# A decoder trunk on one core: at the phase changes of the mix stage, the second tile's opening weights are split right behind the first tile's first product, and the norm's two vectors are loaded in the last phase

## The chip, the cores and the metric

The kernel runs on one core of one Trainium2 chip. The metric is the device time of one execution in microseconds (us). A core has a matrix engine (PE, with its weight loads shown apart as PEld), three other compute engines that work beside it (DVE, ACT, POOL), and queues that start memory transfers; nearly all transfers of this kernel are started by the queue of SP. Each engine takes its instructions in the order in which the built program holds them, and an instruction that waits holds up everything behind it on its engine.

## The reference

One decoder layer on 2048 rows of 1024 float32 values:

```python
u = x * (1.0 + scale) + shift                      # scale, shift, gate from SiLU(c) @ w_ada + b_ada
q, k, v, a_gate, p_in, p_gate, m_a, m_p = split(u @ w_in)
a = (sliding_window_sink_attention(q, k, v) * silu(a_gate)) @ w_attn_proj
p = ((multiscale_causal_pool(p_in) @ w_pool_mix * pool_scale) * silu(p_gate)) @ w_pool_proj
y = (sigmoid(m_a) * a + sigmoid(m_p) * p) @ w_out * (1.0 + gate)
x = layer_norm(alpha * x + y, ln_gain, ln_bias)
```

The last three lines are the kernel's mix stage. `ln_gain` and `ln_bias` are the two vectors of the norm.

## The kernel before

**Products.** A float32 operand is held as two float32r parts: hi, a rounded copy that ACT makes (`CAST`), and lo, the rest, which DVE makes by subtraction (`low`, line 132). A product is hi x hi, hi x lo and lo x hi over four blocks: 12 matmuls of 128x512, the lo part of the weights in the last four. Two by two blocks are multiplied with seven products in place of eight, by sums and differences of blocks: on the activations' side there are seven sets, `B11 T1 T2 B21 T3 B22 T4`, on the weights' side a `Quad`.

**Tiles.** One `Quad` is what the change calls a tile. Its raw weights lie in `W` (four blocks) and `A22`. POOL makes the sums and differences of the blocks in place: `sum1` (line 266) before the first use, `mid` (lines 270 and 271) and `late` (line 275). `pair_split` splits two blocks at once into two buffers `w_set` (cast on line 303, subtraction on line 132). A tile has an opening pair (for the products with `B11` and `T1`), a second pair (for `T2` and `B21`) and a third (for `T3` and `B22`); `half_split` (line 310) does the single block for `T4`. There are four `w_set` buffers, so a pair can be split only when a pair split earlier has been used up by PE.

**Order of the products.** A group is two tiles. `back` does the later products of a group: T2, B21 of tile 1, T2, B21 of tile 2, then T3 and B22 of each, at last T4 of tile 1 and T4 of tile 2. `front` does the opening ones of the next group: B11, T1 of tile 1, B11, T1 of tile 2. Results are drained by DVE a product or two later (`two_behind`).

**Phases.** The mix stage has six: the end of the second half's gates, attention projection and pool projection for the first half of the rows, the same two for the second half, and the output projection with the norm. At each of the five phase changes (called seams 1 to 5 below) the seven sets change as well. `set_steps` loads a set by SP into the lo half of its place, ACT casts it, DVE subtracts (in the profile `set_B<-set_B`, `set_T<-set_T`, 128x1024); `set_steps` gives each step a place in a list counted in products, `hooks` runs it there. So at a seam DVE has three kinds of work: splitting weights, splitting sets, and draining results (`g<-mm,g`, `g<-lg,g`, `wide<-g,wide`, 128x512).

**Who sets the order.** `ring` runs the groups of a phase and calls `after`, which at a seam is the list of two `front` calls that the change replaces; inside a phase the next group's fronts are called in `ring` itself. `tick` runs the hooks and what `defer` put off. Instructions called through `act`, `dve`, `pool`, `sp` and `pe` (the class `Ordered`, line 57 in the profile) keep their written order; those called as `nc.scalar`, `nc.vector`, `nc.gpsimd`, `nc.sync` may be shifted among them by the framework's scheduler, so that one moved call can change more than its own place.

**The norm's vectors.** `vectors` loads gain and bias (512 KB each, spread over 128 partitions) into `wide0` and `wide1`; `hooks` puts it in the last group of phase 4 (the pool projection of the second half). They are first read in `norm_row`'s `power` and `scale`. `load_z` loads rows of x (`in_xr`) to `wide2` to `wide7`.

## Time and profile before

| what | us |
|---|---|
| median of three runs | 1679.81 |
| lowest and highest of them | 1678.58, 1680.28 |
| the profiled execution, its own time | 1682.07 |
| its span, first to last instruction | 1680.3 |
| busy in the span: PE | 1643.7 |
| busy: DVE, ACT, POOL | 1205.1, 1025.5, 957.7 |
| mean granted PE clock (1 is full) | 0.996 |

The mix stage runs from about 1150 us to the end. A row of the timeline gives start, duration, engine, line, operation, written tile and read tiles, shape, count, and in brackets the time that the engine sat idle before it and what ended that. Rows that follow each other are merged where their shapes agree, so one row can stand for several instructions. A duration includes what an instruction lost to others while it ran; the step from one start to the next on a busy engine is what it really took from that engine. A row of the windows view gives for one stretch the time that an engine was busy and how many instructions it began (in brackets), the granted PE clock, the share of time that the 16 transfer engines were busy, and GB/s.

### The profile page before, as it was taken

The page shows a single profiled execution, that of the slowest core. Times are in us where ns is not written, and L with a number is a line of the kernel's source. Part 1 is how long each engine was busy: PE and PEld are TensorE (multiplying, and loading weights), DVE is VectorE, ACT ScalarE, POOL GpSimd, SP SyncE. Part 2 cuts the span into 40 slices and gives each one's busy share as a digit, 9 for nine tenths or more (in the row PEclk, how much of TensorE's full clock was granted, in tenths as well). Part 3 has the DMA queues.
Part 4 walks back from the last instruction along what each step waited for, and adds up shares of the span by engine and source line. Part 5 has one row for each costly group of instructions (what it writes and reads, how often), then busy time and mean ns, then how long its engine had stood idle before and what let it go on. Part 6 is the DMA issues. An engine that isn't in the chain of part 4 may idle for free.

```text
span 1680.3 us, 24675 instructions
## 1 busy us (share of the span) xinstructions
PE 1643.7 (98%) x8058; PEld 1384.1 (82%) x8058; DVE 1205.1 (72%) x2156; ACT 1025.5 (61%) x2146; POOL 957.7 (57%) x710
## 2 busy tenths in 40 slices
PE   7999999999999999999999999999999999999997
PEld 6788888888888788888888888888888878887886
DVE  6944646676867866566567677777769896978777
ACT  4754547778778755334577777776647455544452
POOL 3343437585867838773376858597355563324442
PEclk9999999999999999999999999999999999999999
DMA  9588743243543588872432345335968886677443
GB/s 362 210 295 288 206 156 126 99 127 107 173 137 113 189 269 302 318 270 98 153 128 88 126 131 169 120 126 188 328 229 303 288 310 215 218 261 252 153 148 113
DMA packets 185970, 331.56 MB, mean 197 GB/s; under 512 B 18016, under 2 KB 43760, under 8 KB 185840
## 3 DMA queue, kind: packets, MB, share of 16 engines
q1 hardware_dynamic: 182720, 325.72, 57.0%
q10 hardware_dynamic: 3088, 4.23, 1.1%
q8 instruction: 64, 1.05, 0.3%
q14 instruction: 66, 0.54, 0.1%
q0 software_dynamic: 32, 0.02, 0.0%
HBM read 223.77 MB, written 109.28 MB: 198 GB/s over the span
## 4 chain that ended last, share of the span: by engine, by line
PE 84%; DVE 7%; DMA 4%; issue 2%; ACT 2%; POOL 2%; SPq 0%; POOLq 0%; DVEq 0%; ACTq 0%
PE mm L57 53%; PE lg L57 24%; PE pv L57 4%; PE pt L57 4%; DMA head_T<-in_wada_dram 1%; DVE L L57 1%; DVE w_set L132 1%; DVE set_T L57 1%; DMA head_B<-in_wada_dram 1%; DVE room L57 1%; DMA g<-mp_d 0%; DVE w_set L57 0%; DVE wide L57 0%; ACT L L57 0%; ACT w_set L57 0%
## 5 line engine op out<-in xcount | busy, mean ns | idle before, releaser
L57 PE MATMUL mm<-set_B,w_set 128*128 128x512 f32 x2664 | 654.6, 393 | 5.7 <-DVE w_set L132 5.4
L57 PEld LDWEIGHTS mm<-set_B,w_set 128*128 128x128 f32 x2664 | 496.6, 188 | 108.7 <-DVE w_set L132 6.3
L57 PE MATMUL mm<-set_T,w_set 128*128 128x512 f32 x1824 | 454.9, 396 | 2.1 <-DVE mm L57 1.2
L57 PE MATMUL lg<-set_T,w_set 128*128 128x512 f32 x1704 | 408.6, 390 | 2.1 <-DVE w_set L132 0.6
L57 PEld LDWEIGHTS mm<-set_T,w_set 128*128 128x128 f32 x1824 | 337.6, 189 | 71.5 <-DVE mm L57 4.2
L57 PEld LDWEIGHTS lg<-set_T,w_set 128*128 128x128 f32 x1704 | 318.8, 188 | 70.4 <-DVE w_set L132 1.1
L132 DVE TENSOR_TENSOR w_set<-W,w_set 128x1024 fp32r<-128x1024 f32 x137 | 194.7, 1421 | 145.7 <-ACT w_set L303 136.8
L303 ACT CAST w_set<-W 128x1024 fp32r<-128x1024 f32 x137 | 143.8, 1050 | 194.2 <-PE mm L57 134.2
L57 POOL TENSOR_TENSOR w_set<-W,w_set 128x512 fp32r<-128x512 f32 x120 | 158.9, 1332 | 109.6 <-ACT w_set L57 107.8
L266 POOL TENSOR_TENSOR W<-W,A 128x512 f32<-128x512 f32 x46 | 71.5, 1555 | 261.7 <-DMA A<-in_win_dram 42.8
L57 POOL TENSOR_TENSOR W<-W 128x512 f32<-128x512 f32 x82 | 111.0, 1368 | 52.8 <-DVE sm L57 25.8
L57 DVE TENSOR_TENSOR o<-pv,o 64x128 f32<-64x128 f32 x256 | 71.9, 281 | 96.6 <-ACT o L57 93.2
L270 POOL TENSOR_TENSOR W<-W 128x512 f32<-128x512 f32 x44 | 85.3, 1941 | 96.6 <-DVE w_set L132 75.6
L57 ACT ACTIVATE L<-L,nm 128x257 f32<-128x257 f32 (+1 forms) x256 | 127.2, 498 | 17.8 <-DVE nm L57 8.5
L275 POOL TENSOR_TENSOR W<-W 128x512 f32<-128x512 f32 x46 | 73.1, 1589 | 94.2 <-DVE w_set L132 84.3
L57 DVE CUSTOM_DVE_ANT_0 L<-lg,bt,nsink 128x256 f32<-128x256 f32 (+1 forms) x256 | 111.7, 474 | 15.0 <-DMA pg<-pg_d 10.2
L57 ACT CAST w_set<-W 128x512 fp32r<-128x512 f32 (+1 forms) x165 | 101.5, 629 | 24.5 <-POOL W L57 14.5
L57 ACT COPY o<-pv 64x256 f32<-64x256 f32 x128 | 47.4, 370 | 70.0 <-PE pv L57 68.7
L57 POOL TENSOR_TENSOR spare<-spare 128x512 f32<-128x512 f32 x48 | 84.1, 1760 | 9.4 <-ACT spare L57 7.1
L57 ACT ACTIVATE L<-L,sm 128x256 f32<-128x256 f32 (+1 forms) x128 | 64.3, 502 | 36.9 <-DVE sm L57 36.5
L57 DVE TENSOR_TENSOR ptl<-pt,pth 128x512 fp32r<-128x512 f32 (+1 forms) x128 | 85.7, 669 | 1.0 <-ACT pth L57 0.9
L271 POOL TENSOR_TENSOR W<-W 128x512 f32<-128x512 f32 x44 | 66.8, 1519 | 28.0 <-DMA W<-in_win_dram 20.8
(234 smaller groups left out, 2409.8 us busy)
## 6 DMA issues: line engine op xcount, KB each, us to landing
W<-in_win_dram SPq DMA_DIRECT2D x42, 512.0 KB, 5.9
W<-in_win_dram SPq DMA_DIRECT2D x42, 256.0 KB, 4.1
A<-in_win_dram SPq DMA_DIRECT2D x42, 256.0 KB, 5.0
ag_d<-sig SPq DMA_DIRECT2D x32, 256.0 KB, 5.7
pg_d<-sig SPq DMA_DIRECT2D x32, 256.0 KB, 4.4
pg<-pg_d SPq DMA_DIRECT2D x32, 256.0 KB, 3.4
pin_B<-fin SPq DMA_DIRECT2D x32, 256.0 KB, 2.0
ag<-ag_d SPq DMA_DIRECT2D x32, 256.0 KB, 3.1
```

The lines of the kernel that those rows point to most:

```text
L57: return lambda *args, **kw: self.tc.keep_in_program_order(op(*args, **kw))
L132: engine.tensor_tensor(dst, src, as32(hi), ALU.subtract)
L266: e.tensor_tensor(self.w[:, 1, :], self.w[:, 2, :], self.a22, ALU.add)
L270: e.tensor_tensor(x[:, 1, :], x[:, 1, :], x[:, 0, :], ALU.subtract)
L271: e.tensor_tensor(x[:, 2, :], x[:, 0, :], x[:, 2, :], ALU.subtract)
L275: e.tensor_tensor(x[:, 3, :], x[:, 3, :], x[:, 1, :], ALU.subtract)
L303: a.copy(by_two(hi), raw)
```

## The change

A new function `fronts` takes the place of the two `front` calls at a seam. It hands `front` of tile 1 a function that splits tile 2's opening pair; `front` calls it behind the product with `B11` and ahead of the `tick` that runs that product's hooks. Before, tile 2's pair was split only after both products of tile 1 with both their ticks. The front of tile 2 then takes that pair and makes only its `mid` sums. Fronts inside a phase are as they were.

`vectors` moves from the last group of phase 4 to the output phase, position 3 of its first group, counted in products.

```diff
--- before.py
+++ after.py
@@ -325,11 +325,13 @@
                     skip_group_check=True,
                 )
 
-    def front(ph, q, tick):
-        w = pair_split(ph, q.first())
+    def front(ph, q, tick, w=None, then=None):
+        w = w or pair_split(ph, q.first())
         q.mid()
         a, b = bank(), bank()
         product(a, w[0], "B11", True)
+        if then:
+            then()
         tick()
         product(b, w[1], "T1", True)
         tick()
@@ -412,6 +414,11 @@
             q.consume(ph, 1, 0, c)
         defer(1, lambda: use_up(1))
         defer(2, use_up)
+
+    def fronts(ph, grp, tick):
+        early = []
+        first = front(ph, grp[0], tick, None, lambda: early.append(pair_split(ph, grp[1].first())))
+        return [first, front(ph, grp[1], tick, early[0])]
 
     def finish_pairs(ph, grp, opened, tick):
 
@@ -1621,20 +1628,19 @@
             if i + 1 < len(phases):
                 planned(hooks, ph, phases[i + 1][1], True, groups=groups)
                 nxt = phases[i + 1][0][0]
-                after = lambda tick, nxt=nxt: [front(ph, q, tick) for q in nxt]
+                after = lambda tick, nxt=nxt: fronts(ph, nxt, tick)
             else:
+                def vectors():
+                    for name, src in (("gain", gain), ("lnb", lnb)):
+                        vec[name] = wide(ph, len(vec))
+                        sp.dma_start(vec[name], src.partition_broadcast(P))
+
+                hooks.setdefault((0, 3), []).append(vectors)
                 for at, row in ((1, 2), (1, 3), (5, 4), (5, 5)):
                     hooks.setdefault((0, at), []).append(lambda row=row: load_z(ph, row))
             if i in (3, 5):
                 ta.clear()
             if i == 4:
-
-                def vectors():
-                    for name, src in (("gain", gain), ("lnb", lnb)):
-                        vec[name] = wide(ph, len(vec))
-                        sp.dma_start(vec[name], src.partition_broadcast(P))
-
-                hooks.setdefault((-1, 5), []).append(vectors)
                 hooks.setdefault((-1, 7), []).append(lambda: [load_z(ph, row) for row in range(2)])
             opened = ring(ph, groups, opened, hooks, nxt, after, i == 5)
 
```

What the built program makes of it is shown at three places. The first is DVE at seam 3 (first half's pool projection to second half's attention projection), from the split of the second half of the set T2 on. `w_set` rows are weights: numbers 14055 before and 14027 now are the opening pair of tile 2, 14108 is the second pair of tile 1; `g` and `wide` rows drain results. Before:

```order
L57 TENSOR_TENSOR set_T2_234<-set_T2_234 128x2x512
L57 TENSOR_TENSOR g_13822<-mm_13743,g_13822 128x512
L57 TENSOR_TENSOR wide5_12572<-g_13819,wide5_12572 128x512
L57 TENSOR_TENSOR wide6_12573<-g_13822,wide6_12573 128x512
L57 TENSOR_TENSOR set_B21_68<-set_B21_68 128x2x512
L57 TENSOR_TENSOR g_13824<-lg_13827,g_13824 128x512
L132 TENSOR_TENSOR w_set_14055<-W_13926,w_set_14054 128x1024
L57 TENSOR_TENSOR wide7_12574<-g_13824,wide7_12574 128x512
L57 TENSOR_TENSOR set_B21_68<-set_B21_68 128x2x512
L57 TENSOR_TENSOR set_T3_568<-set_T3_568 128x2x512
L132 TENSOR_TENSOR w_set_14108<-W_13891,w_set_14107 128x1024
```

DVE at the same place now:

```order
L57 TENSOR_TENSOR set_T2_234<-set_T2_234 128x2x512
L57 TENSOR_TENSOR g_13822<-mm_13743,g_13822 128x512
L132 TENSOR_TENSOR w_set_14027<-W_13926,w_set_14026 128x1024
L57 TENSOR_TENSOR wide6_12573<-g_13822,wide6_12573 128x512
L57 TENSOR_TENSOR g_13819<-lg_13782,g_13819 128x512
L57 TENSOR_TENSOR wide5_12572<-g_13819,wide5_12572 128x512
L57 TENSOR_TENSOR set_B21_68<-set_B21_68 128x2x512
L57 TENSOR_TENSOR g_13824<-lg_13827,g_13824 128x512
L132 TENSOR_TENSOR w_set_14108<-W_13891,w_set_14107 128x1024
L57 TENSOR_TENSOR wide7_12574<-g_13824,wide7_12574 128x512
L57 TENSOR_TENSOR set_B21_68<-set_B21_68 128x2x512
```

Tile 2's opening pair now stands ahead of the split of B21's first half, tile 1's second pair ahead of the split of B21's second half and of T3, and the drain of `lg_13782` (before: ahead of this piece) behind the opening pair.

The second place is ACT at the same seam, from the cast of tile 1's opening pair on. Before:

```order
L303 CAST w_set_14006<-W_13891 128x1024
L303 CAST w_set_14054<-W_13926 128x1024
L57 CAST set_B21_68<-set_B21_68 128x2x512
L348 COPY lg_14104<-mm_14012 128x512
L57 CAST set_B21_68<-set_B21_68 128x2x512
L349 COPY p5_14103<-mm_14013 128x512
L303 CAST w_set_14107<-W_13891 128x1024
```

ACT there now:

```order
L303 CAST w_set_14006<-W_13891 128x1024
L303 CAST w_set_14026<-W_13926 128x1024
L57 CAST set_B21_68<-set_B21_68 128x2x512 x2
L303 CAST w_set_14107<-W_13891 128x1024
L350 COPY lg_14104<-mm_14012 128x512
L351 COPY p5_14103<-mm_14013 128x512
```

The cast of tile 1's second pair moved ahead of the two copies; that of tile 2's opening pair already stood ahead of B21. On DVE the rows of seam 5 (pool projection to output projection) read as those of seam 3 do, with `w_set_15253` before and `w_set_15227` now for tile 2's opening pair; on ACT at seam 5 the copy to `lg` stays ahead of the cast of tile 1's second pair, and both now stand behind the two casts of B21.

The third place is SP at seam 5, where `W_15089` and `W_15127` (now `W_15123`) are the output projection's first two tiles, `y_d` the mixed rows in memory, and `A22_15394`, `A22_15441` blocks of the two tiles of its second group. Before:

```order
L255 DMA W_15089<-y_d_137 128x4x128 x3
L57 DMA wide0_15122<-in_gain_dram 128x1024
L57 DMA wide1_15124<-in_lnb_dram 128x1024
L57 DMA y_d_137<-wide4_14505 128x512
L255 DMA W_15127<-y_d_137 128x4x128 x3
L57 DMA y_d_137<-wide6_14538 128x512
L57 DMA wide2_15166<-in_xr_dram 128x1024
L57 DMA wide3_15168<-in_xr_dram 128x1024
```

SP there now:

```order
L255 DMA W_15089<-y_d_137 128x4x128 x3
L255 DMA W_15123<-y_d_137 128x4x128
L57 DMA y_d_137<-wide4_14505 128x512
L255 DMA W_15123<-y_d_137 128x4x128 x2
L255 DMA A22_15394<-y_d_137 128x4x128
L255 DMA A22_15441<-y_d_137 128x4x128
L57 DMA y_d_137<-wide6_14538 128x512
L57 DMA wide2_15162<-in_xr_dram 128x1024
```

Gain and bias left this place, and two loads of the second group's blocks came in. The two vectors now stand behind two loads of rows of x and ahead of the loads of the second group's first tile:

```order
L57 DMA wide4_15327<-in_xr_dram 128x1024
L57 DMA wide5_15329<-in_xr_dram 128x1024
L57 DMA wide0_15370<-in_gain_dram 128x1024
L57 DMA wide1_15372<-in_lnb_dram 128x1024
L255 DMA W_15393<-y_d_137 128x4x128 x3
```

On PE and POOL the order of the instructions is the same before and now.

## The prediction

> **What bounds the kernel now.** I read the page's head first, then the chain of waits, the waits of PE, the windows around each wait, and the timeline of the seams.

> ```profile
> span 1680.3 us, 24675 instructions
> PE 1643.7 (98%) x8058; PEld 1384.1 (82%) x8058; DVE 1205.1 (72%) x2156; ACT 1025.5 (61%) x2146; POOL 957.7 (57%) x710
> ```

> PE is busy 98% of the span, so this change can pay only where PE waits in the mix stage or runs slowly. PE's timeline shows three waits at the stretches that the change touches:

> ```profile
> 1227.55 1.21 PE L57 MATMUL lg<-set_T,w_set 128*128 128x512 f32 x4 [0.64 <-DVE w_set L132]
> 1366.21 1.98 PE L57 MATMUL mm<-set_B,w_set 128*128 128x512 f32 x4 [2.33 <-DVE w_set L132]
> 1523.51 2.07 PE L57 MATMUL mm<-set_B,w_set 128*128 128x512 f32 x4 [3.08 <-DVE w_set L132]
> ```

> The second is seam 3, the third seam 5. Both times PE has done eight matmuls of tile 2's first product and waits for the lo part of that tile's opening pair. Seams 1, 2 and 4 show no wait there; the 0.64 comes later in seam 1's group. The windows of PE say what a wait leaves behind (after the count comes the granted clock, then the transfer share):

> ```profile
> 1226.00:1227.50 1.50, 0.90 (x4) 1.00 0.00 0
> 1366.20:1368.00 1.80, 1.79 (x5) 0.54 1.03 381
> 1369.00:1370.00 1.00, 1.00 (x5) 0.63 1.01 342
> 1370.00:1371.00 1.00, 1.00 (x6) 1.00 1.06 408
> 1523.50:1525.00 1.50, 1.50 (x4) 0.50 1.02 325
> 1525.00:1527.00 2.00, 2.00 (x7) 0.56 0.87 259
> ```

> After each long wait PE runs at half clock for some 3 us; the wait of 0.64 leaves the clock at 1.00 in its window. The chain has the price:

> ```profile
> 1366.21 5.52 PE mm L57 x16
> 1371.73 2.72 PE lg L57 x12
> 1523.51 5.45 PE mm L57 x16
> ```

> Twelve matmuls take 2.72 at full clock, or 0.227 each, so sixteen take 3.63, and the two stretches lost 1.89 and 1.82 more.

> **Part 1: tile 2's opening pair, split earlier.** Seam 3 before, on DVE, ACT, PE and POOL:

> ```profile
> 1353.88 1.21 DVE L132 TENSOR_TENSOR w_set<-W,w_set 128x1024 fp32r<-128x1024 f32 x1
> 1353.99 1.05 ACT L303 CAST w_set<-W 128x1024 fp32r<-128x1024 f32 x1 [2.57 <-DVE g L57]
> 1355.18 1.68 POOL L270 TENSOR_TENSOR W<-W 128x512 f32<-128x512 f32 x1 [1.77 <-DVE w_set L132]
> 1355.62 0.68 DVE L57 TENSOR_TENSOR g<-mm,g 128x512 f32<-128x512 f32 x1
> 1361.33 1.06 ACT L57 CAST set_B<-set_B 128x1024 fp32r<-128x1024 f32 x1 [6.28 <-DMA set_B<-ain_B]
> 1361.40 0.68 DVE L57 TENSOR_TENSOR g<-mm,g 128x512 f32<-128x512 f32 x1
> 1361.91 1.98 PE L57 MATMUL mm<-set_B,w_set 128*128 128x512 f32 x8
> 1363.20 1.22 DVE L57 TENSOR_TENSOR set_B<-set_B 128x1024 fp32r<-128x1024 f32 x1
> 1364.94 1.21 DVE L132 TENSOR_TENSOR w_set<-W,w_set 128x1024 fp32r<-128x1024 f32 x1
> 1366.30 6.15 POOL L270 TENSOR_TENSOR W<-W 128x512 f32<-128x512 f32 x1 [9.44 <-DVE w_set L132]
> 1368.95 1.22 DVE L132 TENSOR_TENSOR w_set<-W,w_set 128x1024 fp32r<-128x1024 f32 x1
> ```

> The cast of the pair is done by 1355 (second row); only its subtraction, at 1364.94, is late: it stands behind six drains and the split of B21, whose cast waited for a transfer until 1361.33. In the new order it follows the drain that was at 1361.40. Rows of 128x1024 step by 1.14, rows of 128x512 by 0.60. Two drains that stood ahead of that one now stand behind it or one place on, so I put it 0.6 earlier, at 1360.8, or at worst where it was. The subtraction then ends at 1362.0 to 1362.6. PE wants it at 1361.91 + 8 x 0.227 = 1363.7. The wait of 2.33 goes, and the half clock behind it.

> Can what follows keep up with a PE that is 4.2 us earlier? T2 of tile 1 would start at 1361.91 + 24 x 0.227 = 1367.35 and want the lo part of its pair at 1369.2. DVE in the new order, from 1362.6: two drains and `lg` to 1364.4, half of B21 and a drain to 1366.1, that pair to 1367.3. The margin is 1.9. Then a drain, half of B21 to 1369.0 (wanted about 1371), both halves of T3 to 1371.3, tile 2's second pair to 1372.5, wanted at 1372.8 + 1.8 = 1374.6. That pair also needs POOL's `mid`, which took 6.15 at 1366.30 since DVE ran four rows of two on-chip operands without a gap; at 1355.18, with a drain from the accumulators (`g<-mm`) behind, it took 1.68. In the new order it starts at 1362.6 with the drain of `lg` next, so I take 1.7; even 6.15 would end at 1368.8, before DVE asks. POOL's sum puts about 1.2 on DVE each time that it gets in between. Two such sums leave margins near zero, so I deduct 0.5.

> Seam 5 has the same picture:

> ```profile
> 1511.80 1.21 DVE L132 TENSOR_TENSOR w_set<-W,w_set 128x1024 fp32r<-128x1024 f32 x1
> 1518.07 0.58 ACT L348 COPY lg<-mm 128x512 f32<-128x512 f32 x1
> 1518.45 1.97 PE L57 MATMUL mm<-set_B,w_set 128*128 128x512 f32 x8
> 1518.70 0.68 DVE L57 TENSOR_TENSOR g<-mm,g 128x512 f32<-128x512 f32 x1
> 1522.24 1.21 DVE L132 TENSOR_TENSOR w_set<-W,w_set 128x1024 fp32r<-128x1024 f32 x1
> ```

> The subtraction moves from 1522.24 to behind the drain of 1518.70, which itself comes 0.6 earlier: it ends by 1519.9, and PE wants it at 1518.45 + 1.8 = 1520.3. Here the drain of `lg` moves behind it, to about 1520.4, and ACT's copy to `lg` (1518.07 before) must wait for that drain, until 1521.1 or, with a POOL sum between, 1521.7; behind it on ACT stands the cast of tile 1's second pair, done by 1522.7. T2 would start at 1518.45 + 5.45 = 1523.9, its lo part be wanted at 1525.7 and be done at 1524.5 to 1525.2. Tile 2's second pair is done at 1529.7 to 1531.5 and wanted at 1531.1. Again 0.5 is deducted.

> Seams 1, 2 and 4 have no wait to lose. At seam 1 the pair's cast depends on POOL:

> ```profile
> 1203.63 2.31 DVE L57 TENSOR_TENSOR set_B<-set_B 128x1024 fp32r<-128x1024 f32 x1
> 1204.88 1.05 ACT L303 CAST w_set<-W 128x1024 fp32r<-128x1024 f32 x1 [1.12 <-POOL W L266]
> 1205.97 2.21 DVE L132 TENSOR_TENSOR w_set<-W,w_set 128x1024 fp32r<-128x1024 f32 x1
> ```

> In the new order the split of B21 (first row) stands behind the third row, so DVE idles from 1203.63 to 1205.97, 2.34 us. POOL then works unhindered: both rows last twice their 1.2, so about two POOL sums fall out of DVE's way, 2.3 in return. I take 0, between a gain of the 0.64 and a loss of 2.34. Seams 2 and 4 swap a split and a drain of 0.6 to 1.1, hidden by the fact that PE has no wait there; 0, within 0.6 either way.

> **Part 2: the vectors.** Removed from seam 5 are two issues on SP and their two transfers. The first row is of the chain, the others of the timeline:

> ```profile
> 1497.18 6.32 DMA wide<-in_gain_dram
> ...
> 1497.18 1.31 SPq L57 DMA_DIRECT2D wide<-in_gain_dram  x1
> 1498.54 0.45 SPq L57 DMA_DIRECT2D wide<-in_lnb_dram  x1
> 1502.56 2.73 DVE L132 TENSOR_TENSOR w_set<-A,w_set 128x512 fp32r<-128x512 f32 x2 [0.83 <-ACT w_set L310]
> 1525.96 1.93 SPq L57 DMA_DIRECT2D wide<-in_xr_dram  x2
> 1537.44 0.38 SPq L255 DMA_DIRECT2D W<-y_d  x1
> 1551.43 1.64 DVE L57 SCALAR_TENSOR_TENSOR wide<-wide,mean,wide 128x1024 f32<-128x1024 f32 x1
> ```

> Tile 2's raw weights land earlier, but DVE's row at 1522.24 shows its split late by DVE's own queue and not for want of them: 0. The two block loads that come into this place wait for buffers that DVE frees by 1502.56 + 2.73 = 1505.3, before the store queued next is due: 0. The vectors are issued behind the rows of x, near 1528, and land by 1541 if each takes the 6.3 that the chain gave gain; their first reader comes at 1551.43 - 4.9 = 1546.5. The second group's weights behind them (1537.44) wait for a buffer, not for SP. 0, at worst 1.31 + 0.45 = 1.8.

> **Sum.** 2.33 + 1.89 + 3.08 + 1.82 = 9.1, less 1.0 deducted: 8.1 off. The profiled execution took 1682.07 for a span of 1680.3; it would take 1674.0. The median of the runs shown, 1679.81, lies 2.26 below it, and becomes 1671.7.

> [...] The rows above show the clock halved after waits of 2.33 and 3.08. [...]

> **Rivals.**

> *The waits turn into short ones.* DVE's amount of work is unchanged. If its rows finish no earlier than before, tile 1's second pair is done at 1370.2 and 1527.4, against 1369.2 and 1525.7 wanted: waits of 1.0 and 1.7, short of 2.33. Gain 9.1 - 2.7 = 6.4, or 4.6 if the 1.7 costs clock: 1673.4 to 1675.2. Against it: that pair now stands two or three rows earlier.

> *Nothing to measure.* The transfers, not DVE, set the pace: their share is 1.0 from 1366 on, and a PE that is earlier meets sets that are not. The pull is given back before the seam's group ends: within 3.4 of 1679.81, 1676.4 or more. Against it: with the share at 1.0 PE has no wait between seam 3 and seam 5 in the rows above, and B21's cast ran at 1361.33, nine us ahead of its product.

> *The half clock is not due to the wait.* If the saturated transfers caused it, only 5.4 - 1.0 = 4.4 would go: 1675.4. Against it: at 1370 the share is 1.06 and the clock 1.00.

> [...]

> *Slower.* ACT and DVE take instructions in order, and the early split now heads both queues; where tile 2's sums are late, as at seam 1, everything behind it waits. Price per seam: the idle 2.34 passed on to PE, and 1.9 of clock, 4.2. At seams 1, 2 and 4 together 12.6, less 9.1: 3.5 slower, 1683.3. It decides when all three bite. Only seam 1 shows a late sum.

> **Chances.** A difference under 0.2% (3.4 us) can hardly be told from none. Both waits gone: 0.56, the forecast 1671.7. Short waits: 0.20. Clock unchanged: 0.03. Nothing to measure: 0.12. Slower: 0.09. So faster 0.79, same 0.12, slower 0.09. The range reaches from 1669.3 (all 9.1, and the 0.64, and some scatter) to 1677.0, which takes in the short waits and the edge of no change.

> **What would show it.** Right: PE's waits of 2.33 and 3.08 absent, granted clock 1.00 at both seams, the subtraction of tile 2's opening pair ahead of that of B21, POOL's `mid` near 1.7. Wrong: a new wait of 2 us or more of PE for the second pair or for B21 in the same groups; at seam 1 the 0.64 grown; norm rows waiting for gain.

## The result

| | median, us | lowest and highest | ratio to the kernel before, with its 95% interval |
|---|---|---|---|
| changed kernel, six runs | 1673.78 | 1672.59, 1676.22 | 0.9965 (0.9952 to 0.9977) |
| the same again, five runs | 1675.20 | 1673.98, 1675.91 | 0.9967 (0.9955 to 0.9980) |
| the same once more, six runs | 1674.84 | 1673.96, 1676.78 | 0.9967 (0.9954 to 0.9979) |

Each row was taken beside runs of the kernel before on the same chip, with medians of 1680.12, 1680.26 and 1681.03. So the change makes the kernel faster by 5.1 to 6.3 us, 0.33 to 0.35%. The forecast was 1671.7 with a range of 1669.3 to 1677.0. The profiled execution of the changed kernel took 1675.67 for a span of 1673.9 us.

The profile after: the timeline of seam 3, on DVE, PE, POOL and the weight loads.

```profile
1361.87 1.22 DVE L132 TENSOR_TENSOR w_set<-W,w_set 128x1024 fp32r<-128x1024 f32 x1
1362.70 2.88 PE L57 MATMUL mm<-set_B,w_set 128*128 128x512 f32 x12
1363.17 1.70 POOL L270 TENSOR_TENSOR W<-W 128x512 f32<-128x512 f32 x1 [5.96 <-DVE w_set L132]
...
1367.07 1.21 DVE L132 TENSOR_TENSOR w_set<-W,w_set 128x1024 fp32r<-128x1024 f32 x1
...
1373.32 2.30 DVE L132 TENSOR_TENSOR w_set<-W,w_set 128x1024 fp32r<-128x1024 f32 x1
...
1375.67 0.77 PEld L57 LDWEIGHTS lg<-set_T,w_set 128*128 128x128 f32 x4 [0.54 <-DVE w_set L132]
```

The subtraction of tile 2's opening pair starts at 1361.87 (1364.94 before), and PE runs tile 2's first product as one row of twelve: the wait of 2.33 is gone. POOL's `mid` behind it takes 1.70 in place of 6.15. What is late next is tile 2's second pair (1373.32, where it took 2.30 beside a POOL sum of 2.36, in place of 1.21): the weight loads wait 0.54 for it. At seam 5 the same rows read:

```profile
1515.54 1.22 DVE L132 TENSOR_TENSOR w_set<-W,w_set 128x1024 fp32r<-128x1024 f32 x1
1516.83 1.68 POOL L270 TENSOR_TENSOR W<-W 128x512 f32<-128x512 f32 x1 [5.36 <-DVE w_set L132]
...
1528.24 0.77 PEld L57 LDWEIGHTS lg<-set_T,w_set 128*128 128x128 f32 x4 [0.34 <-DVE w_set L132]
```

And the windows of PE over both seams (time busy, instructions, granted clock, transfer share, GB/s) show no idle time and no half clock, at a transfer share of 1.0:

```profile
1365.00:1373.00 8.00, 8.00 (x37) 1.00 1.04 393
1523.00:1530.00 7.00, 7.00 (x32) 1.00 1.00 333
```

**Where the time went.** PE executes the same instructions in the same order in both kernels, so the start of the same instruction in the two traces tells what was won or lost up to there. Five such rows of PE's timeline, of the kernel before (the start of the mix stage, ahead of and behind seam 3, and the two ends of the output projection's second group):

```profile
1151.58 0.96 PE L57 MATMUL mm<-set_T,w_set 128*128 128x512 f32 x3 [0.45 <-DVE sm L57]
1318.39 2.88 PE L57 MATMUL mm<-set_B,w_set 128*128 128x512 f32 x12
1398.77 2.88 PE L57 MATMUL mm<-set_B,w_set 128*128 128x512 f32 x12
1556.00 2.88 PE L57 MATMUL mm<-set_B,w_set 128*128 128x512 f32 x12
1594.08 2.88 PE L57 MATMUL mm<-set_B,w_set 128*128 128x512 f32 x12
```

The same five of the changed kernel:

```profile
1153.11 0.97 PE L57 MATMUL mm<-set_T,w_set 128*128 128x512 f32 x3 [0.45 <-DVE sm L57]
1319.18 2.88 PE L57 MATMUL mm<-set_B,w_set 128*128 128x512 f32 x12
1395.79 2.88 PE L57 MATMUL mm<-set_B,w_set 128*128 128x512 f32 x12
1548.81 2.88 PE L57 MATMUL mm<-set_B,w_set 128*128 128x512 f32 x12
1587.66 2.88 PE L57 MATMUL mm<-set_B,w_set 128*128 128x512 f32 x12
```

Row by row the changed kernel stands at +1.53, +0.79, -2.98, -7.19 and -6.42. It enters the mix stage 1.53 late (a matter of stages that the change does not touch, see the clock below), wins 0.74 up to seam 3, all of it around seam 1, then 3.77 at seam 3 and 4.21 at seam 5, and loses 0.77 again in the second group of the output projection. In the mix stage that is 7.95, where 8.1 was forecast; the profiles of the second and third row of the table give 7.80 and 6.91. What takes the 0.77, on PE and DVE of the changed kernel:

```profile
1556.64 1.28 DVE L57 SCALAR_TENSOR_TENSOR wide<-wide,rs,wide 128x1024 f32<-128x1024 f32 x1 [1.57 <-POOL rs L57]
...
1560.83 1.22 DVE L132 TENSOR_TENSOR w_set<-W,w_set 128x1024 fp32r<-128x1024 f32 x1
...
1562.10 1.21 PE L57 MATMUL lg<-set_T,w_set 128*128 128x512 f32 x4 [0.44 <-DVE rs L57]
```

DVE sits idle 1.57 for a norm row's `rs`, which POOL raises to a power; behind that in DVE's order stands the second pair of the next group, and PE waits for it. The kernel before has the same idle time on DVE (1.58), but there PE was later and the chain was in time.

### The profile page after: what moved, and what is told of

Its sections match the earlier page's. It is cut to its first block, busy times and chain, and to the rows that moved or that the text cites. A ratio compares the mean times of both kernels' runs of the same rounds, so it can differ in the third digit from the quotient of the medians.

```text
span 1673.9 us, 24680 instructions
## 1 busy us (share of the span) xinstructions
PE 1642.9 (98%) x8058; PEld 1383.7 (83%) x8058; DVE 1205.2 (72%) x2156; ACT 1024.4 (61%) x2146; POOL 947.1 (57%) x710
## 3 DMA queue, kind: packets, MB, share of 16 engines
q8 instruction: 64, 1.05, 0.3%
## 4 chain that ended last, share of the span: by engine, by line
PE 84%; DVE 6%; DMA 4%; POOL 2%; issue 2%; ACT 2%; SPq 0%; POOLq 0%; DVEq 0%; ACTq 0%
PE mm L57 53%; PE lg L57 24%; PE pv L57 4%; PE pt L57 4%; DMA head_T<-in_wada_dram 1%; DVE w_set L132 1%; DMA set_T<-ain_T 1%; DVE wide L57 1%; DMA head_B<-in_wada_dram 1%; DVE set_T L57 1%; DVE L L57 1%; DVE w_set L57 0%; ACT L L57 0%; ACT w_set L57 0%; POOL W L270 0%
## 5 line engine op out<-in xcount | busy, mean ns | idle before, releaser
L57 PE MATMUL mm<-set_B,w_set 128*128 128x512 f32 x2664 | 652.1, 392 | 0.1
L57 PEld LDWEIGHTS mm<-set_B,w_set 128*128 128x128 f32 x2664 | 495.9, 188 | 101.9 <-DVE set_B L57 0.7
L57 PE MATMUL mm<-set_T,w_set 128*128 128x512 f32 x1824 | 454.9, 396 | 1.6 <-DVE mm L57 1.2
L57 PE MATMUL lg<-set_T,w_set 128*128 128x512 f32 x1704 | 409.7, 390 | 2.1 <-ACT set_T L57 0.5
L57 PEld LDWEIGHTS mm<-set_T,w_set 128*128 128x128 f32 x1824 | 337.5, 189 | 70.5 <-DVE mm L57 3.3
L57 PEld LDWEIGHTS lg<-set_T,w_set 128*128 128x128 f32 x1704 | 318.4, 188 | 71.9 <-DVE w_set L132 1.6
L132 DVE TENSOR_TENSOR w_set<-W,w_set 128x1024 fp32r<-128x1024 f32 x137 | 194.7, 1423 | 143.9 <-ACT w_set L303 135.3
L303 ACT CAST w_set<-W 128x1024 fp32r<-128x1024 f32 x137 | 144.0, 1051 | 186.2 <-PE mm L57 130.2
L266 POOL TENSOR_TENSOR W<-W,A 128x512 f32<-128x512 f32 x46 | 73.7, 1603 | 260.0 <-DMA A<-in_win_dram 63.6
L57 POOL TENSOR_TENSOR w_set<-W,w_set 128x512 fp32r<-128x512 f32 x120 | 159.0, 1333 | 109.2 <-ACT w_set L57 104.4
L57 DVE TENSOR_TENSOR o<-pv,o 64x128 f32<-64x128 f32 x256 | 72.0, 281 | 96.9 <-ACT o L57 93.6
L57 POOL TENSOR_TENSOR W<-W 128x512 f32<-128x512 f32 x82 | 110.9, 1366 | 52.4 <-DVE sm L57 25.4
L57 ACT ACTIVATE L<-L,nm 128x257 f32<-128x257 f32 (+1 forms) x256 | 127.1, 498 | 18.4 <-DVE nm L57 8.9
L275 POOL TENSOR_TENSOR W<-W 128x512 f32<-128x512 f32 x46 | 70.8, 1540 | 112.3 <-DVE w_set L132 97.6
L270 POOL TENSOR_TENSOR W<-W 128x512 f32<-128x512 f32 x44 | 77.4, 1763 | 83.1 <-DVE w_set L132 70.9
L57 DVE CUSTOM_DVE_ANT_0 L<-lg,bt,nsink 128x256 f32<-128x256 f32 (+1 forms) x256 | 111.6, 473 | 14.4 <-DMA pg<-pg_d 5.1
L57 ACT CAST w_set<-W 128x512 fp32r<-128x512 f32 (+1 forms) x165 | 101.4, 628 | 25.1 <-POOL W L57 14.5
L57 ACT COPY o<-pv 64x256 f32<-64x256 f32 x128 | 47.3, 369 | 71.7 <-PE pv L57 70.5
L57 POOL TENSOR_TENSOR spare<-spare 128x512 f32<-128x512 f32 x48 | 82.8, 1732 | 10.1 <-ACT spare L57 5.8
L57 DVE TENSOR_TENSOR ptl<-pt,pth 128x512 fp32r<-128x512 f32 (+1 forms) x128 | 85.7, 669 | 1.0 <-ACT pth L57 0.9
L57 ACT ACTIVATE L<-L,sm 128x256 f32<-128x256 f32 (+1 forms) x128 | 64.3, 502 | 36.0 <-DVE sm L57 35.6
L271 POOL TENSOR_TENSOR W<-W 128x512 f32<-128x512 f32 x44 | 68.1, 1548 | 29.2 <-DMA W<-in_win_dram 22.0
```

Source lines behind the costliest of these rows:

```text
L57: return lambda *args, **kw: self.tc.keep_in_program_order(op(*args, **kw))
L132: engine.tensor_tensor(dst, src, as32(hi), ALU.subtract)
L266: e.tensor_tensor(self.w[:, 1, :], self.w[:, 2, :], self.a22, ALU.add)
L270: e.tensor_tensor(x[:, 1, :], x[:, 1, :], x[:, 0, :], ALU.subtract)
L271: e.tensor_tensor(x[:, 2, :], x[:, 0, :], x[:, 2, :], ALU.subtract)
L275: e.tensor_tensor(x[:, 3, :], x[:, 3, :], x[:, 1, :], ALU.subtract)
```

## The experiments

Three theories were set against each other. The two waits (the forecast's theory): PE's waits of 2.33 and 3.08 at seams 3 and 5, and the half clock behind them, are the gain. The vectors: moving them gives a part of it. Blocking: the early split holds up the in-order queues at seams 1, 2 and 4 and costs there. In the tables below, "seam 1", "seam 3" and "seam 5" are what a kernel's profiled execution won against that of the kernel before between the rows of PE shown above (seam 5 from 1431.41 to 1556.00), and "second group" what it lost from 1556.00 to 1594.08. They are taken from unrounded starts, so they can differ by 0.01 from the rows shown.

### The parts of the change alone

Split alone, vectors at the old place (in full the change without its last hunk):

```diff
-                hooks.setdefault((0, 3), []).append(vectors)
...
+                hooks.setdefault((-1, 5), []).append(vectors)
```

> The change without the moved vectors: `fronts` at all five seams, gain and bias loaded where they were before. Theory (the two long waits of PE and the half clock behind them are the whole gain): as the changed kernel, 6 to 8 us below the kernel before, PE's waits of 2.33 (seam 3) and 3.08 (seam 5) absent, the 0.64 at seam 1 absent. Rival (moving the vectors frees SP's queue and the transfers at seam 5): 1 to 2 us of the gain are missing, since SP is again held for 1.31 + 0.45 us at seam 5, and a wait of PE of 1 us or more stands there.

Vectors alone:

```diff
-                after = lambda tick, nxt=nxt: fronts(ph, nxt, tick)
+                after = lambda tick, nxt=nxt: [front(ph, q, tick) for q in nxt]
```

> The moved vectors without the early split. Theory of the two waits: within 1 us of the kernel before; PE's waits of about 2.3 and 3.1 for the opening pair's lo part stay, and PE runs at about half clock behind both. Rival (the vectors): seam 5's wait shrinks by up to 1.8 us and its half clock with it, 1.5 to 3 us faster. If the new place of the vectors cost something, the norm's rows at the first group of the output projection would wait for gain, and the kernel would be slower by that wait.

Early split at seams 3 and 5 alone, vectors moved:

```diff
-                after = lambda tick, nxt=nxt: fronts(ph, nxt, tick)
+                after = lambda tick, nxt=nxt, i=i: fronts(ph, nxt, tick) if i + 1 in (3, 5) else [front(ph, q, tick) for q in nxt]
```

> Early split at seams 3 and 5 alone, vectors moved. Theory of the two waits: 3.8 at seam 3 and 3.4 at seam 5 by the traces of the two kernels, so 7.2 below the kernel before less the scatter of about 1, some 0.7 above the changed kernel at most, because the 0.64 at seam 1 is back. Rival (the early split blocks the in-order queues where it finds no wait, at seams 1, 2 and 4, and costs there): 1 us or more below the changed kernel, 8 us or more below the kernel before.

Early split at seams 1, 2 and 4 alone (`in (1, 2, 4)` in the same line), vectors at the old place:

> Early split at seams 1, 2 and 4 alone, vectors at the old place. Theory of the two waits: the waits of 2.33 and 3.08 stay with their half clock; the 0.64 at seam 1 goes; 0 to 1 us below the kernel before. Rival (blocking at these seams): slower by 1 to 4 us at each seam where it bites, with a new wait of PE at seam 1, 2 or 4.

| kernel | median, us | ratio (95% interval) | seam 1 | seam 3 | seam 5 | second group |
|---|---|---|---|---|---|---|
| changed, first profile | 1673.78 | 0.9965 (0.9952 to 0.9977) | 0.73 | 3.78 | 4.21 | 0.77 |
| split alone | 1676.33 | 0.9971 (0.9960 to 0.9982) | 0.59 | 2.70 | 4.46 | 2.24 |
| vectors alone | 1680.26 | 0.9997 (0.9988 to 1.0006) | 0.12 | 0.25 | 0.22 | 0.00 |
| seams 3 and 5 | 1674.25 | 0.9963 (0.9950 to 0.9976) | 1.00 | 3.15 | 4.21 | 1.15 |
| seams 1, 2, 4 | 1680.63 | 1.0001 (0.9991 to 1.0010) | 0.28 | 0.78 | 0.17 | 0.00 |

The kernel before had a median of 1680.55 beside the last four. Seams 3 and 5, with the vectors moved, give all of it, seams 1, 2 and 4 nothing that can be measured. The theory of the two waits holds, blocking falls. The 0.73 around seam 1 is not the split either, since the kernel without an early split there wins 1.00. It is PE's wait of 0.64 in that group, which comes and goes whatever the edit: it is absent from all three profiles of the changed kernel and from that of seams 3 and 5, 0.40 in the seams 1, 2 and 4 kernel, and 0.69 in the second run of the split alone below, both of which split early there. With the vectors alone the waits stand as before, in PE's timeline:

```profile
1366.19 2.08 PE L57 MATMUL mm<-set_B,w_set 128*128 128x512 f32 x4 [2.14 <-DVE w_set L132]
...
1523.24 2.07 PE L57 MATMUL mm<-set_B,w_set 128*128 128x512 f32 x4 [2.90 <-DVE w_set L132]
```

By this run the vectors give nothing, but the split alone came out 2.5 above the changed kernel; by the two profiles 1.47 of that is lost in the second group and 1.08 at seam 3. That was not expected.

### Do the vectors have a part after all?

> The changed kernel once more, beside the next three on one chip. Theory (the two long waits, with a chance part from the granted clock): 1673 to 1676 us; the profile shows no wait of PE over 1 us between seam 2 and seam 5. Whether the clock is halved near 568 us, behind the waits of 1.39 and 0.63 of the unchanged attention stage, is left to chance: about one profile in two.

> The early split without the moved vectors, once more beside the changed kernel. If the 2.5 us between this kernel and the changed one are scatter (a wait of 1.50 for a transfer at 827 us and a halved clock, both in stages that the edit does not touch): within 1 us of the changed kernel. If moving the vectors has a part of its own, once DVE is the one that is late behind seam 5: 1.5 to 3 us above the changed kernel, with waits of PE over 1 us in all in the second group of the output projection (1.52 in the first trace, 0.44 in that of the changed kernel).

Beside each other on one chip the changed kernel had 1675.20 and the split alone 1677.18 (1675.59 to 1678.21, eleven runs; ratio 0.9979, 0.9970 to 0.9987): 2.0 more, again. The trace puts it in the second group: lost there are 3.01, against 0.54 in the changed kernel's second profile. PE's timeline of the split alone:

```profile
1561.45 2.11 PE L57 MATMUL lg<-set_T,w_set 128*128 128x512 f32 x8 [1.28 <-ACT w_set L303]
1564.62 1.20 PE L57 MATMUL lg<-set_T,w_set 128*128 128x512 f32 x4 [1.06 <-DVE rs L57]
```

So the vectors have a part, about 2 us, but only together with the split: alone, that group has slack (0.00 lost). By what way? Moving them let two `A22` loads of that second group go 35 and 38 us earlier on SP (1500.45 and 1502.16, against 1535.50 and 1540.09 with the split alone). The scheduler also put a copy and a cast on ACT and a drain on DVE, between 1522 and 1531, in another place; no run here undoes that. The next kernel undoes the earlier loads alone, by sending them through the queue in written order; DVE, ACT, PE and POOL keep the order of the changed kernel:

```diff
-                    q.dma_start(dst.rearrange("p (k q) -> p k q", k=4), self.srcs[src][:, 4 * half : 4 * half + 4, :])
+                    (sp if dst is self.a22 and self.ordered else q).dma_start(dst.rearrange("p (k q) -> p k q", k=4), self.srcs[src][:, 4 * half : 4 * half + 4, :])
...
-        outs = [out_quad(k) for k in range(0, S // P, 2)]
+        outs = [out_quad(k) for k in range(0, S // P, 2)]; outs[2].ordered = outs[3].ordered = True
```

> The changed kernel, as the measure for the next two on the same chip: 1673 to 1676 us, no wait of PE over 1 us between seam 2 and the end.

> The changed kernel with one thing undone: on SP, the two `A22` loads of the output projection's second group stand behind their `W` loads again, as they do with the vectors at the old place (1535.5 and 1540.1 in that trace), in place of ahead of seam 5's stores; every other engine's order is that of the changed kernel, and gain and bias stay at their new place. Theory A (what the vectors' move gives, about 2 us, it gives by letting these two blocks land early, so that POOL's `sum1` of the second group does not wait for them): 1.5 to 2.5 us above the changed kernel, with waits of PE of 1.2 and 1.0 in the second group, as in the two runs of the split alone. Theory B (it gives by taking 1 MB of vectors out of the transfers ahead of seam 5): within 0.5 us of the changed kernel, waits in that group 0.5 or less.

It had 1675.84 (1674.95 to 1676.70, seven runs; ratio 0.9972, 0.9962 to 0.9983) beside 1674.84 for the changed kernel. One us is between what A and B expect, and the runs overlap, so the times decide nothing. The traces say more. POOL's `sum1` of the second group's second tile in this kernel waits for its `A22` block, which landed at 1544.85, 0.85 behind the block of `W`:

```profile
1545.01 1.30 POOL L266 TENSOR_TENSOR W<-W,A 128x512 f32<-128x512 f32 x1 [3.98 <-DMA A<-y_d]
```

What a late `sum1` does is seen in two profiles of the changed kernel, in which `A22` is there long before and `sum1` needs only the block of `W`. In the first profile that block landed at 1543.89. The `mid` sum behind `sum1` on POOL is done before DVE splits the group's opening pair:

```profile
1545.86 1.29 POOL L271 TENSOR_TENSOR W<-W 128x512 f32<-128x512 f32 x1
1548.16 1.21 DVE L132 TENSOR_TENSOR w_set<-W,w_set 128x1024 fp32r<-128x1024 f32 x1
```

In the third profile PE is 1.25 earlier in that group, but the block landed only at 1544.66. The two rows then overlap, they take 2.15 in place of 1.29 and 2.31 in place of 1.21, and the power of the norm row, next on POOL, comes 0.75 behind the group's first product in place of 1.69 ahead of it:

```profile
1544.82 1.29 POOL L266 TENSOR_TENSOR W<-W,A 128x512 f32<-128x512 f32 x1 [4.83 <-DMA W<-y_d]
1546.19 2.15 POOL L271 TENSOR_TENSOR W<-W 128x512 f32<-128x512 f32 x1
1547.11 2.31 DVE L132 TENSOR_TENSOR w_set<-W,w_set 128x1024 fp32r<-128x1024 f32 x1
...
1562.49 1.19 PE L57 MATMUL lg<-set_T,w_set 128*128 128x512 f32 x4 [1.03 <-DVE rs L57]
```

All eight profiles that have the early split at seam 5 and the norm's steps at their old places fall into these two cases (the group's first product is the one at 1548.81 in the first profile; "T3 later" is described in the next part):

| profile | `sum1` starts ahead of the group's first product | split of the opening pair | lost in the second group |
|---|---|---|---|
| changed, first | 4.76 | 1.21 | 0.77 |
| changed, second | 5.79 | 1.22 | 0.54 |
| changed, third | 2.74 | 2.31 | 2.39 |
| split alone, first | 2.89 | 2.32 | 2.24 |
| split alone, second | 2.07 | 2.31 | 3.01 |
| seams 3 and 5 | 5.20 | 1.22 | 1.15 |
| blocks in order | 3.49 | 2.32 | 1.67 |
| T3 later | 5.35 | 1.21 | 0.25 |

Where `sum1` starts 4.76 or more ahead, 0.25 to 1.15 is lost; where it starts 3.49 or less ahead, 1.67 to 3.01. With the split alone `A22` landed 2.14 and 0.88 behind the block of `W`. In the first of these two profiles that alone made `sum1` late: by the block of `W` it could have started 5.0 ahead. That is theory A's way. In the second the block of `W` was late already (3.0 ahead), as it is in the third profile of the changed kernel. Theory B's sign, waits of 0.5 or less, failed too in the run made for it, which has a wait of 1.05. So the larger loss goes with a late `sum1`, but how much of the 2 us is due to `A22` stays open.

### The short waits that remain

Sets of T3 split one product later, so that tile 2's second pair does not stand behind them:

```diff
-    SPLIT_AT = (2, 3, 4, 5, 8, 9, 11, 12, 13, 14, 15, 16, 17, 18)
+    SPLIT_AT = (2, 3, 4, 5, 8, 9, 11, 12, 14, 15, 15, 16, 17, 18)
```

> The changed kernel with the splits of the set T3 one product later, so that tile 2's second pair does not stand behind them on DVE at the seams. Theory (the short waits that remain at seams 3 and 5 are DVE's order, not its amount of work): the weight loads' waits of 0.54 at seam 3 and 0.34 + 0.35 + 0.34 at seam 5 shrink to 0.3 or less in all, 1 us below the changed kernel, within scatter. Rival (DVE has too little time there in whatever order): the waits come back for T3 itself, and the time is that of the changed kernel or up to 1 us above.

The same, and the norm's `scale` one product later:

```diff
-            for at, f in ((1, sums), (2, squares), (3, power), (4, scale), (6, store)):
+            for at, f in ((1, sums), (2, squares), (3, power), (5, scale), (6, store)):
```

> The kernel before this one, and in the output projection the last step of a norm row (`scale`, which waits for POOL's power) put off by one more product, so that DVE does not sit idle for POOL with the next group's second pair behind it. Theory (the wait of 0.44 for `rs` in the second group, with the rest of the 1.4 us that seam 5's gain loses by there, is DVE waiting for POOL's result in order): PE's waits in that group go, another 0.5 to 1.5 us below. Rival (DVE is late there by its backlog from seam 5): no change, and the wait is then for the weights.

The later `scale` alone:

> The changed kernel with the norm's `scale` one product later and the sets as they were. Theory (the later sets of T3 only moved the waits at the seams; the later `scale` took the waits of the second output group away): 0.5 to 1.5 us below the changed kernel, waits at seams 3 and 5 as in the changed kernel, none in the second output group, and the fastest of all. Rival (the gain of that pair of edits was scatter): within 0.5 us of the changed kernel.

| kernel | median, us | the changed kernel beside it | ratio to before (95% interval) | seam 3 | seam 5 | second group |
|---|---|---|---|---|---|---|
| T3 later | 1675.71 | 1675.20 | 0.9971 (0.9959 to 0.9983) | 1.89 | 3.97 | 0.25 |
| T3 and `scale` later | 1674.08 | 1675.20 | 0.9961 (0.9949 to 0.9974) | 2.52 | 4.17 | 0.00 |
| `scale` later | 1672.95 | 1674.84 | 0.9957 (0.9945 to 0.9970) | 3.85 | 4.76 | 0.00 |

T3 later is a miss, as its rival said: DVE has too little time there in whatever order. The wait only goes to a later pair and grows, in PE's timeline of that kernel:

```profile
1380.84 1.20 PE L57 MATMUL lg<-set_T,w_set 128*128 128x512 f32 x4 [1.18 <-DVE w_set L132]
```

The later `scale` does what it should. In its timeline the pair on DVE no longer stands behind the step that waits for POOL, and PE's product runs through:

```profile
1551.73 1.21 DVE L132 TENSOR_TENSOR w_set<-W,w_set 128x1024 fp32r<-128x1024 f32 x1
1552.86 1.27 DVE L57 SCALAR_TENSOR_TENSOR wide<-wide,rs,wide 128x1024 f32<-128x1024 f32 x1
...
1556.42 1.21 DVE L132 TENSOR_TENSOR w_set<-W,w_set 128x1024 fp32r<-128x1024 f32 x1
...
1557.99 2.88 PE L57 MATMUL lg<-set_T,w_set 128*128 128x512 f32 x12
```

The changed kernel with the later `scale` has the lowest median of all kernels here, 1.9 under the changed kernel on the same chip (runs 1672.65 to 1674.19 against 1673.96 to 1676.78), and loses nothing in the second group, though PE comes to it 8.89 earlier than before. So the loss that was left there comes from the norm row's chain over POOL with the next group's weights behind it on DVE, and not from DVE having too much to do. The edit moved two things, however: in the built program POOL's power of the next norm row now also stands ahead of a `mid` sum (at 1549.97, ahead of the sum at 1553.09), where in the changed kernel it stood behind it (1556.05, behind a sum of 2.33 at 1553.77). Which of the two moves gives how much is not shown. In both profiles with a later `scale` the `sum1` above starts early (4.90 and 5.02 ahead), so it is not shown either what the edit does for the larger loss behind a late `sum1`.

### What makes the clock fall

In the trace of the seams 1, 2 and 4 kernel the wait at seam 3 was 2.43, longer than before, and the clock stayed at 1.00. Its windows of PE around seam 3:

```profile
1361.34:1364.76 3.42, 2.62 (x12) 1.00 1.12 406
1364.76:1368.17 3.41, 1.78 (x8) 1.00 0.98 299
1368.17:1371.58 3.41, 3.41 (x17) 1.00 1.05 386
```

The kernel before, around seam 3 and behind the wait of seam 5:

```profile
1362.92:1366.34 3.42, 1.09 (x6) 1.00 1.00 347
1366.34:1369.75 3.41, 3.41 (x9) 0.50 1.04 354
1369.75:1373.16 3.41, 3.41 (x17) 1.00 1.05 404
...
1523.35:1526.76 3.41, 3.25 (x8) 0.50 0.95 293
```

The two stretches at half clock of the kernel before (the second and the last row) are 3.41 us long each and start 1523.35 - 1366.34 = 157.01 apart, 46 times 3.413. So in this execution they lie on a grid of 3.41 us, and the windows above are laid on it: where PE idled 2.33 in one window of the grid, the next ran at half clock; where a wait of 2.43 lay across two (0.80 and 1.64 idle), none did. To test this away from the saturated seams, waits were put in at seven places inside phases (the result stays the same):

```diff
-        low(d, by_two(lo), raw, by_two(hi))
+        for _ in range(1 + again):
+            low(d, by_two(lo), raw, by_two(hi))
...
+    late = [5, 4, 2, 5, 3, 5, 1]
...
-                opened = [front(ph, q, tick) for q in groups[gi + 1]]
+                more = late.pop(0) if late and ph.name == "mix" else 0
+                opened = [front(ph, q, tick, again=more * (x == 0)) for x, q in enumerate(groups[gi + 1])]
```

> The changed kernel with waits of PE put in at seven places inside the phases of the mix stage, away from the seams: the lo part of tile 1's opening pair is computed 5, 4, 2, 5, 3, 5 and 1 times more (the same result), which should make PE wait 1.1, 1.6, 1.7, 2.3, 2.1, 2.7 and 1.1 us there, at a transfer share of 0.4 to 0.8. Theory W (the clock is set in windows of 3.41 us on a grid that runs through; a window in which PE idles for more than about half makes the next one run at half clock, which costs 1.7): half clock for exactly 3.41 behind those waits that leave over 1.7 idle in one window of the grid, none behind those that lie across two windows or are shorter. Theory R (only a window that is idle throughout makes the clock fall): no half clock behind any of them. Theory D (half clock needs saturated transfers): none either, since the share is below 0.9.

It took 1715.81. At the first six places PE waited 3.59, 5.12, 1.35, 6.34, 5.65 and 7.20, mostly longer than aimed at, at the seventh not at all. Windows of PE on the grid of that run:

```profile
1245.24:1248.65 3.41, 0.92 (x4) 1.00 0.00 0
1248.65:1252.07 3.42, 3.42 (x10) 0.50 0.00 0
1252.07:1255.48 3.41, 3.41 (x16) 1.00 0.00 0
1409.08:1412.49 3.41, 2.06 (x9) 1.00 0.00 0
1412.49:1415.91 3.42, 3.42 (x16) 1.00 0.03 5
1327.16:1330.57 3.41, 0.00 (x0) 1.00 0.88 286
1330.57:1333.98 3.41, 3.06 (x7) 0.50 0.12 44
1487.59:1491.00 3.41, 0.58 (x3) 1.00 0.20 77
1491.00:1494.41 3.41, 0.00 (x0) 0.50 0.00 0
1494.41:1497.82 3.41, 3.30 (x8) 0.50 0.18 68
1617.29:1620.71 3.42, 1.66 (x8) 1.00 0.38 153
1620.71:1624.12 3.41, 0.00 (x0) 1.00 0.00 0
1624.12:1627.53 3.41, 1.38 (x3) 0.50 0.00 0
```

The stretches at half clock in these rows start at 1248.65, 1330.57, 1491.00 and 1624.12: 81.92, 160.43 and 133.12 apart, 24, 47 and 39 times 3.413, again on a grid. The first window idles for 2.49 of its 3.41, with not one transfer running, and the next is at half clock: D is out, and so is R, since PE was busy for 0.92 of that window. An idle 1.35 left the clock alone, and the wait of 7.20 at the sixth place (the last three rows are its first windows) brought half clock only behind the window that it fills, not behind the one in which it begins with 1.76. Of 37 windows on the grid, from five profiles (before, two of the changed kernel, seams 1, 2 and 4, and this run), nine idled for 2.03 to 3.41, and each of them was followed by half clock; six idled for 1.35 to 1.76, and one was; the others idled for 0.80 or less, and none was whose next is among the 37. In these windows theory W holds, but without its sharp edge at 1.7 us: in between, the idle time alone did not decide, since a window with 1.76 idle was not followed by half clock (first of the last three rows) and one with 1.39 was (below).

This also explains the 1.53 by which the changed kernel entered the mix stage late: 0.9 of it is half clock behind such a window near 568 us in the attention stage, behind two waits that both kernels have (1.39 and 0.63 in the changed kernel). Two profiles of the changed kernel, first the first:

```profile
566.27:569.68 3.41, 2.02 (x13) 1.00 0.11 38
569.68:573.09 3.41, 3.41 (x11) 0.50 0.78 286
```

and the second, where another window with the same idle time brought no half clock:

```profile
563.29:566.70 3.41, 2.01 (x10) 1.00 0.88 333
566.70:570.12 3.42, 2.76 (x16) 1.00 0.21 76
```

Half clock near 568 us is in the first profiles of the changed kernel and of the split alone and in that of the vectors alone (a granted clock of 0.89 and 0.87 from 560 to 570 us in the last two), and not in those of the kernel before, the changed kernel's second, seams 3 and 5, and seams 1, 2 and 4. Another 0.8 is lost at 828.75, also in a part that the change does not touch, where PE waits 0.87 for a transfer; that wait was 1.50 in the first profile of the split alone, and the profile of the kernel before does not have it.

## Why the prediction was right, and where it was off

**The likeliest case came true.** Both waits are gone, the granted clock is 1.00 at both seams, the subtraction ends at 1361.87 + 1.22 = 1363.1 (forecast 1362.0 to 1362.6) where PE, itself 0.8 later than reckoned, wants it at 1362.70 + 8 x 0.227 = 1364.5, and `mid` takes 1.70 (1.7 forecast). Seams 3 and 5, with the vectors moved, give the whole gain. One reading was loose: between the cast, done at 1355.04, and the subtraction DVE has ten drains and three halves of sets, and not six drains and B21. Nothing hangs on it, since the sum went by the drain at 1361.40 alone.

**Seam 3** was sized 2.33 + 1.89 - 0.5 = 3.72; the three profiles of the changed kernel show 3.78, 2.98 and 3.51, so that the first comes so close is in part luck. The deduction of 0.5 was for short waits behind POOL's sums, and they came: tile 2's second pair was waited for 0.54 by the weight loads in the first profile, and 0.42 and 0.34 by PE in the others.

**Seam 5** was sized 3.08 + 1.82 - 0.5 = 4.40; up to the second output group it gave 4.21, 4.59 and 4.79 in the three profiles, and 3.44, 4.05 and 2.40 with it. The mis-sized term is the deduction: it looked for short waits in seam 5's own group, and put nothing aside for the next one. There DVE, with the same work and a PE that is 7 to 8 us earlier, meets the norm rows' chain over ACT and POOL, and that group gave back 0.77, 0.54 and 2.39. The run with a later `scale` loses nothing there, which shows the chain to be the cause of the two smaller losses; in the third profile the late `sum1` comes on top.

**Seams 1, 2 and 4** were put at 0, and are 0: a ratio of 1.0001 (0.9991 to 1.0010) with the split there alone. The rival that the early split would block the queues fell with it: the idle time that it priced came (DVE sat idle 2.27 at seam 1, 2.34 reckoned), and PE did not wait for it. What the trace shows won around seam 1 comes without the split too.

**The vectors** were put at 0, at worst 1.8 dearer. Alone they are 0 (ratio 0.9997). In the changed kernel they are not: at the old place the split costs 2.0 and 2.5 more. The step that failed is the one that put the two block loads in their place at 0: it asked what those loads cost where they now stand, and not what it is worth to the second output group to have the blocks early. With PE earlier, that group has no slack left for a late block, as the table of eight profiles shows; how much of the 2 us these two blocks make stays open.

**The clock.** That the half clock is due to the waits held: a window with PE idle for 2.33 was followed by it, and one with 2.49 and no transfer running too. The rival with the clock unchanged starts from 5.4, which is the two waits alone, 2.33 + 3.08; the first profile won 3.78 and 4.21 at the two seams. But the prediction took the price of the clock as certain. Of the six waits of 2.1 to 3.1 at seams 3 and 5 (in the kernel before, vectors alone, and seams 1, 2 and 4) five were followed by half clock; one lay across two windows of the grid and was not.

**The rest of the distance.** The median came out 2.1 to 3.5 above the forecast, though the mix stage of the first profile won 7.95 of the 8.1. Three things together are of the right size. The medians of the kernel before beside the three rows of the result lie 0.3 to 1.2 above the 1679.81 that the sum started from. The second output group gave back 1.23 in the mean of three profiles. And the sum was made against one execution of the kernel before with half clock at both seams, while others had less of it: the granted clock of 52 other runs of that kernel is 0.994 to 0.998, in the mean 0.9959, and that of the 17 runs of the changed kernel 0.9975. Taken off the span, the clock costs 6.8 us in the one and 4.1 in the other (with half clock in which PE had nothing to do), so the change won 2.7 by the clock in the mean, where the sum has 1.89 + 1.82 = 3.71. This is an estimate: the other runs have a mean clock, but no profile.

## What to carry to other kernels

A wait that is taken off one engine makes that engine early for all that follows: look for the next chain of fixed length that it now runs into, here a norm step that waits for another engine's result with the next weights queued behind it, and move that step as well. A part of a change that is worth nothing alone can be worth a third of the gain or more beside the other part, so parts are tried both alone and left out. The cost of a wait of PE was here its length and, behind five of six waits of 2.1 to 3.1 us, a stretch of half clock (1.89 and 1.82 more in the kernel before): one profile shows one throw of it.

## What was not expected of the hardware

POOL's in-place sum of 128x512 took 6.15 us beside four DVE rows of 128x1024 without a gap that read two on-chip operands and took their usual 1.22 each, and 1.70 in the new order, with three rows of 128x512 on DVE beside it: at the same size it took 3.6 times as long with the one set of DVE rows as with the other. It was not POOL alone that took longer in every case: at 1372.18 in the changed kernel a POOL sum took 2.36, and the DVE row beside it 2.30.
